# End of the up-projection: two chunks' biases and taps back to back, and the lows of down's second and third pair by subtraction instead of an accumulating transfer

## The chip, the cores and the metric

The kernel runs on one core of one Trainium2 chip. The metric is the device time of one execution in microseconds (us); for a comparison, the median of several runs. The engines are written as in the profile: PE is TensorE's matmul, PEld its weight load, DVE is VectorE, ACT is ScalarE, POOL is GpSimd, SP is SyncE, which here only issues DMAs.

## The reference

A decoder trunk of two layers over x of 512 tokens by 1024 features, in float32. Each layer is a mixer (dilated window attention in the first, forgetting attention in the second) and then a gated feed-forward block with a causal convolution. The change lies in that block, which runs once a layer:

```python
def conv_ffn(xn, w_up, cw, cb, w_down):       # w_up 1024 x 5632, w_down 2816 x 1024
    a = xn @ w_up
    T = a.shape[1]
    ap = jnp.pad(a, ((0, 0), (CONV_W - 1, 0), (0, 0)))           # CONV_W = 3
    a = sum(ap[:, j:j + T] * cw[j] for j in range(CONV_W)) + cb
    gate, val = jnp.split(a, 2, axis=-1)
    return (jax.nn.gelu(gate, approximate=True) * val) @ w_down
...
h = h + rms_norm(conv_ffn(rms_norm(h, g[2]), w_up[l], conv_w[l], conv_b[l], w_down[l]), g[3])
```

## The kernel before

**Products in two halves.** TensorE works on float32 numbers split in two: a *high* (the number rounded, made by a cast on ACT, `act.copy`) and a *low* (the number less its high). A product is three matmuls, high by high, high by low and low by high: lines 295, 296 and 297, in `mm3`. A low comes about in one of two ways. Either DVE subtracts the high from the raw tile (`pair_lows`, L836). Or ACT writes the negated rounded number (a scaled copy, L829) and POOL issues a DMA that adds the raw tile to it in place (L830).

**Up-projection.** The 5632 output features are 22 chunks of 128 gate features and 128 value features. Chunks 4 to 19 go in pairs by a scheme with seven products instead of eight; chunks 0 to 3, 20 and 21 go alone (`up`). A chunk's two results lie in two of the eight PSUM banks (`bank`, name "up"). Then, on the bank's results: ACT adds bias and the last tap (`biased` L657, or in `taps` L670), DVE adds the two other taps, two instructions for the gate and two for the value (`shifted`, L664), ACT takes the GELU of the gate (`glu`, L689), and POOL multiplies gate and value (`product`, L686) and stores the product in `hD` in DRAM. `product()` always works on the chunk whose GELU was issued last before it.

**Down-projection.** Its 22 chunks of input form 11 pairs, again in a scheme with seven products. For a pair j, `pair_load` fetches the stored products, `pair_sums` makes three sums of them on DVE (L817 to L819) and stores one, `pair_highs` makes three highs on ACT (L827; two tiles of weights "wraw" and one of activations "dact"), and `pair_lows` the three lows. `mul_one(j, bp)` is twelve matmuls into four banks (name "acc"). `down` runs pairs 0 and 1 for bp = 0, then for bp = 1, then pair 2, pair 3 and so on with both: 24 matmuls a pair. The first four "acc" banks are those of chunks 18 and 19, the next four those of chunks 20 and 21; a bank is free when DVE has made the last tap from it.

**What sets the order.** Each engine runs its own instructions in the order in which the code issues them, and waits for other engines by semaphores. The code of `ffn` is written in the order that is wanted. Pair 0 is prepared during the last chunks in pairs (`prepare_last`); pairs 1 and 2 between the products of the last two chunks, in the lines that the change touches; pair 3 and the later ones in `down`. In what follows "sums(2)" or "lows(1)" are the steps of `pair_sums(2)` and `pair_lows(1)`, and "taps 18" the four instructions of L664 for chunk 18.

Of the kernel before, what the change touches and what calls it, by code (L numbers as in the profile page):

```python
# [12 lines left out]
AF = mybir.ActivationFunctionType  # L13
ALU = mybir.AluOpType
# [7 lines left out]
NF = DFF // 128  # L22
# [93 lines left out]
def trunk_kernel(ctx, tc, x, norm_gains, w_qkv_a, w_o_a, w_q_b, w_o_b, kv_norm, w_kvf, b_f,  # L116
                 w_up, conv_w, conv_b, w_down, rope, out):
    nc = tc.nc
    act, dve, pool, pe, sp = nc.scalar, nc.vector, nc.gpsimd, nc.tensor, nc.sync
# [8 lines left out]
    def t8(shape, dt=F32, name="t8"):  # L128
        return p8.tile(shape, dt, tag="t8", name=name)

    def t4(shape, dt=F32, name="t4"):
        return p4.tile(shape, dt, tag="t4", name=name)

    def t2(shape, dt=F32, name="t2"):
        return p2.tile(shape, dt, tag="t2", name=name)

    def bank(shape, name="bank"):
        return psp.tile(shape, F32, tag="ps", name=name)
# [510 lines left out]
    def ffn(l, bd, cp, nxt, ahead):  # L649
# [4 lines left out]
        def biased(c, banks):  # L654
            bb = t4([128, 2, T], name="bb")
            for s, ch in ((0, c), (1, NF + c)):
                act.activation(bb[:, s, :], banks[s], AF.Identity, bias=cp[:, 3, ch:ch + 1],  # L657
                               scale=cp[:, 2, ch:ch + 1])
            return bb

        def shifted(c, banks, bb, s):
            ps, ch = banks[s], s * NF + c
            for n in (1, 2):
                dve.scalar_tensor_tensor(bb[:, s, n:], ps[:, :T - n], cp[:, 2 - n, ch:ch + 1], bb[:, s, n:],  # L664
                                         ALU.mult, ALU.add)

        def taps(c, banks, between=None):
            bb = t4([128, 2, T], name="bb")
            for s, ch in ((0, c), (1, NF + c)):
                act.activation(bb[:, s, :], banks[s], AF.Identity, bias=cp[:, 3, ch:ch + 1],  # L670
                               scale=cp[:, 2, ch:ch + 1])
                shifted(c, banks, bb, s)
                if s == 0 and between is not None:
                    between()
            return bb
# [3 lines left out]
        def product():  # L679

            if gated:
                c, bb = gated.pop()
                if c - 1 in hc:
                    pool.dma_start(hD[c - 1], hc.pop(c - 1))
                hc[c] = t2([128, T], name="hc")
                pool.tensor_tensor(hc[c], bb[:, 0, :], bb[:, 1, :], ALU.mult)  # L686

        def glu(c, bb):
            act.activation(bb[:, 0, :], bb[:, 0, :], AF.Gelu_apprx_tanh)  # L689
            gated.append((c, bb))  # L690

        def post(c, banks, between=None):
            product()
            glu(c, taps(c, banks, between))
# [90 lines left out]
        def prepare_last():  # L785

            for added in (False, True, False, False):
                W.high(added)
                (W.low_added if added else W.low)()
                yield  # L790
            pair_sums(0)
            yield
            pair_highs(0)
            pair_sums(1)
            yield
            pair_lows(0)
            yield
# [1 line left out]

        acts, one, two, raws, todo, later2 = {}, {}, {}, {}, {}, {}
        H = slice(0, 512), slice(512, 1024)
        a11, s1_, s3_, s2_ = (slice(i * 256, i * 256 + 256) for i in range(4))

        def pair_load(j):

            if j < ND:
                acts[j] = k = t8([128, 1024], name="dact")
                sp.dma_start(k[:, 0:512], hD[2 * j])  # L810
                sp.dma_start(k[:, s2_], hD[2 * j + 1, :, 256:512])

        def pair_sums(j):

            pair_load(j + 1)
            k = acts[j]
            dve.tensor_tensor(k[:, s3_], k[:, a11], k[:, s1_], ALU.subtract)  # L817
            dve.tensor_tensor(k[:, s1_], k[:, s1_], k[:, s2_], ALU.add)
            dve.tensor_tensor(k[:, s2_], k[:, s1_], k[:, a11], ALU.subtract)  # L819
            pool.dma_start(sD[j], k[:, s2_])  # L820

        def pair_highs(j, added=False):

            raws[j] = [*W.take(2), acts.pop(j)]
            one[j] = [t8([128, 2, 1024], F32R, name="w") for _ in range(3)]
            for w, r in zip(one[j], raws[j]):
                act.copy(w[:, 0], r)  # L827
                if added and r is not raws[j][2]:
                    act.activation(w[:, 1], r, AF.Copy, scale=-1.0)  # L829
                    pool.dma_start(w[:, 1], r, accum_op=ALU.add)  # L830
            todo[j] = slice(2 if added else 0, 3)

        def pair_lows(j):
            s = todo.pop(j)
            for w, r in zip(one[j][s], raws.pop(j)[s]):
                dve.tensor_tensor(w[:, 1], r, w[:, 0].bitcast(F32), ALU.subtract)  # L836

        def load_two(j):
# [68 lines left out]

        def down(nxt, ahead):
            pair_highs(3)
            for bp in range(2):  # L910
                for j in range(2):
                    mul_one(j, bp)
            for j in range(1, ND - 2):
                if j > 1:
                    mul_one(j, 0)
                    mul_one(j, 1)
                if j + 3 < ND:
                    pair_sums(j + 3)
                    pair_lows(j + 2)
                    pair_highs(j + 3)  # L920
                elif j + 3 == ND:
                    pair_lows(j + 2)
                    load_two(0)
# [58 lines left out]
        def up(w, o, kcs):  # L982
            wh, wl = (t.rearrange("p (k c) -> p k c", k=8) for t in w)
            for kc in kcs:
                bh, bl = xs(xT, kc, ALL)
                mm3(o, wh[:, kc, :], wl[:, kc, :], bh, bl, kc == 0, kc == KD - 1)
# [16 lines left out]
        before = None  # L1003
        for c in (2, 3):
            banks = [bank([128, T], name="up") for _ in range(2)]
            for s in range(2):
                up(W.get(), banks[s], range(KD))
                if s == 0 and before:
                    product()
                    bb = taps(*before)  # L1010
# [8 lines left out]
            before = c, banks  # L1019
# [10 lines left out]
        def begin(p):  # L1030

            banks = [[bank([128, T], name="up") for _ in range(2)] for _ in range(2)]
            times(p, "A11", [b[0][:, LO] for b in banks], True)
            return banks

        def keep_first(banks):
            s1 = t2([128, 2, 256], name="csum")
            for q, b in enumerate(banks):
                act.copy(s1[:, q], b[0][:, LO])
            return s1  # L1040
# [8 lines left out]
        pend = [(*before, 0, None, None)]  # L1049
        banks = begin(PAIRS[0])  # L1050
        s1 = keep_first(banks)
        for p in PAIRS:
# [16 lines left out]
            bbs = [biased(*pend[0][:2])]  # L1069
# [34 lines left out]
            pend = [(2 * p + q, banks[q], q, s1, s12) for q in range(2)]  # L1104
            if p + 1 in PAIRS:
                banks, s1 = later, keep_first(later)
# [3 lines left out]
        banks = [begun[1], bank([128, T], name="up")]  # L1110
# [1 line left out]
        begun = None  # L1112
        ends(pend)
        product()
        glu(pend[0][0], taps(*pend[0][:2]))
        pair_highs(1, True)
        up(W.get(), banks[1], range(KD))
        post(*pend[1][:2])
        pair_sums(2)
        before = NF - 2, banks  # L1120
        banks = [bank([128, T], name="up") for _ in range(2)]
        up(W.get(), banks[0], range(KD))
        product()
        glu(before[0], taps(*before, lambda: pair_lows(1)))
        up(W.get(), banks[1], range(KD))
        before = NF - 1, banks
        pair_highs(2, True)
        post(*before)
        pair_lows(2)
        pair_sums(3)  # L1130
        product()
# [443 lines left out]

    bd2 = SharedBoundary(load_gain(norm_gains[0, 3], "gain03"), gcol, "xk")
    ffn(0, bd, cp[0], bd2, 4)


# [69 lines left out]
    banks = {b: bank([128, 512], name="v_ps") for b in bd2.order}  # L1649
# [78 lines left out]
    banks = [bank([128, 512], name="v_ps") for _ in range(4)]  # L1728
# [131 lines left out]
    for n in range(N + 3):  # L1860
        live = n < N
        if live:
            j, i = units[n]
# [53 lines left out]


    ffn(1, bd, cp, Final(load_gain(norm_gains[1, 3], "gain13")), 0)


# [40 lines left out]
```

## Time and profile before

| what | value |
|---|---|
| median of 3 runs | 1095.73 us (1094.23 to 1095.74) |
| the profiled execution | 1095.56 us |
| its span, first to last instruction | 1093.8 us |
| mean granted TensorE clock over the span | 0.997 |
| busy: PE, PEld | 1082.7 us (99%), 958.0 us (88%) |
| busy: DVE, ACT, POOL | 888.1 us (81%), 703.5 us (64%), 320.7 us (29%) |
| end of the up-projection, first and second layer | about 386 to 402 us and 965 to 979 us from the span's start |

The page of the profile gives each engine's busy time as a share of the span. The other views used below are the list of waits (who waited for whom, how long in all, how often, the longest), the timeline of an engine (start, length, instruction, and in brackets the idle time before it with what ended it), and a table of busy times by stretches of time. Matmuls are pipelined, so their lengths overlap; the distance between two starts tells their pace. The TensorE clock is given as a share of the full one.

### The profile page before, as it was taken

The page shows a single profiled execution, that of the slowest core. Times are in us where ns is not written, and L with a number is a line of the kernel's source. Part 1 is how long each engine was busy: PE and PEld are TensorE (multiplying, and loading weights), DVE is VectorE, ACT ScalarE, POOL GpSimd, SP SyncE. Part 2 cuts the span into 40 slices and gives each one's busy share as a digit, 9 for nine tenths or more (in the row PEclk, how much of TensorE's full clock was granted, in tenths as well). Part 3 has the DMA queues.
Part 4 walks back from the last instruction along what each step waited for, and adds up shares of the span by engine and source line. Part 5 has one row for each costly group of instructions (what it writes and reads, how often), then busy time and mean ns, then how long its engine had stood idle before and what let it go on. Part 6 is the DMA issues. An engine that isn't in the chain of part 4 may idle for free.

```text
span 1093.8 us, 18994 instructions
## 1 busy us (share of the span) xinstructions
PE 1082.7 (99%) x6897; PEld 958.0 (88%) x6897; DVE 888.1 (81%) x1442; ACT 703.5 (64%) x1155; POOL 320.7 (29%) x338
## 2 busy tenths in 40 slices
PE   9999999999999999999999999999999999999997
PEld 7888889899999977888888888889899999987886
DVE  5898978679899879997686677858679999879995
ACT  6745666766776666576551677756766676757573
POOL 2643000364665542000001212100354565532000
PEclk9999999999999999999999999999999999999999
DMA  9899956898788989793447857775898788989862
GB/s 291 242 364 411 349 127 158 187 213 223 195 200 230 267 255 343 274 343 96 154 133 246 277 167 209 254 223 142 172 226 206 216 190 214 250 276 328 319 250 77
DMA packets 162677, 254.25 MB, mean 232 GB/s; under 512 B 13216, under 2 KB 106776, under 8 KB 162584
## 3 DMA queue, kind: packets, MB, share of 16 engines
q1 hardware_dynamic: 143784, 189.33, 52.1%
q0 software_dynamic: 18112, 63.71, 26.6%
q8 instruction: 54, 0.88, 0.3%
q14 instruction: 39, 0.32, 0.1%
q10 hardware_dynamic: 688, 0.01, 0.0%
HBM read 172.37 MB, written 39.73 MB: 194 GB/s over the span
## 4 chain that ended last, share of the span: by engine, by line
PE 90%; DMA 3%; issue 2%; ACT 2%; DVE 2%; POOL 1%; SPq 0%; DVEq 0%; ACTq 0%; POOLq 0%
PE up L295 11%; PE up L297 11%; PE up L296 11%; PE acc L295 8%; PE acc L297 8%; PE acc L296 8%; PE v_ps L295 2%; PE v_ps L296 2%; PE v_ps L297 2%; PE pT_ps L1803 2%; PE o_ps L1818 2%; PE s_ps L1769 2%; PE qk_ps L295 1%; PE first L295 1%; PE first L296 1%
## 5 line engine op out<-in xcount | busy, mean ns | idle before, releaser
L295 PE MATMUL up<-xsh,w 128*128 128x256 f32 x512 | 145.0, 283 | 0.0
L296 PE MATMUL up<-xsl,w 128*128 128x256 f32 x512 | 145.0, 283 | 0.0
L297 PE MATMUL up<-xsh,w 128*128 128x256 f32 x512 | 145.0, 283 | 0.0
L664 DVE SCALAR_TENSOR_TENSOR bb<-up,conv,bb 128x511 f32<-128x511 f32 (+1 forms) x160 | 118.6, 746 | 28.0 <-ACT bb L670 25.2
L736 ACT CAST w<-wraw 128x1024 fp32r<-128x1024 f32 x94 | 95.4, 1043 | 66.1 <-DVE wraw L764 44.8
L295 PE MATMUL acc<-w 128*128 128x512 f32 (+1 forms) x311 | 121.5, 391 | 3.1 <-DVE bb L664 3.1
L297 PE MATMUL acc<-w 128*128 128x512 f32 (+1 forms) x311 | 121.3, 390 | 0.3 <-DVE w L836 0.3
L296 PE MATMUL acc<-w 128*128 128x512 f32 (+1 forms) x267 | 104.1, 390 | 0.5 <-DMA w<-wraw 0.5
L686 POOL TENSOR_TENSOR hc<-bb 128x512 f32<-128x512 f32 x44 | 79.0, 1796 | 68.1 <-DVE bb L664 54.3
L297 PEld LDWEIGHTS up<-xsh,w 128*128 128x128 f32 x512 | 98.3, 192 | 0.0
L295 PEld LDWEIGHTS up<-xsh,w 128*128 128x128 f32 x512 | 98.3, 192 | 0.0
L296 PEld LDWEIGHTS up<-xsl,w 128*128 128x128 f32 x512 | 98.3, 192 | 0.0
L296 PE MATMUL up<-xbl,w 128*128 128x256 f32 (+1 forms) x256 | 79.3, 310 | 0.0
L295 PE MATMUL up<-xbh,w 128*128 128x256 f32 (+1 forms) x256 | 79.3, 310 | 0.0
L296 PE MATMUL up<-xcl,w 128*128 128x256 f32 (+1 forms) x256 | 79.3, 310 | 0.0
L295 PE MATMUL up<-xch,w 128*128 128x256 f32 (+1 forms) x256 | 79.3, 310 | 0.0
L297 PE MATMUL up<-xbh,w 128*128 128x256 f32 (+1 forms) x256 | 79.3, 310 | 0.0
L297 PE MATMUL up<-xch,w 128*128 128x256 f32 (+1 forms) x256 | 79.3, 310 | 0.0
L76 DVE TENSOR_TENSOR w<-wraw,w 128x1024 fp32r<-128x1024 f32 x50 | 60.1, 1221 | 17.6 <-ACT w L58 13.3
L58 ACT CAST w<-wraw 128x1024 fp32r<-128x1024 f32 x61 | 62.8, 1054 | 17.5 <-PE v_ps L296 6.9
L295 PEld LDWEIGHTS acc<-w 128*128 128x128 f32 x311 | 58.8, 189 | 16.4 <-issue 2.9
L297 PEld LDWEIGHTS acc<-w 128*128 128x128 f32 x311 | 58.8, 189 | 12.8 <-DVE w L836 0.7
(314 smaller groups left out, 3189.9 us busy)
## 6 DMA issues: line engine op xcount, KB each, us to landing
wraw<-in_w_up_dram SPq DMA_DIRECT2D x88, 512.0 KB
w<-wraw POOLq DMA_DIRECT2D x70, 512.0 KB, 5.2
dT<-dsums SPq DMA_DIRECT2D x28, 512.0 KB
dsums<-in_w_down_dram SPq DMA_DIRECT2D x22, 512.0 KB
dsums<-in_w_down_dram SPq DMA_DIRECT2D x44, 256.0 KB
hD<-hc POOLq DMA_DIRECT2D x44, 256.0 KB, 6.4
dact<-hD SPq DMA_DIRECT2D x44, 256.0 KB
wraw<-dT SPq DMA_DIRECT2D x22, 512.0 KB
```

The costliest lines, as they stand in the source:

```text
L58: (copy or self.nc.scalar.copy)(pair[:, 0], raw)
L76: self.nc.vector.tensor_tensor(pair[:, 1], raw, pair[:, 0].bitcast(F32), ALU.subtract)
L295: pe.matmul(o, ah, bh, start=first, stop=False, skip_group_check=shared)
L296: pe.matmul(o, ah, bl, start=False, stop=False, skip_group_check=shared)
L297: pe.matmul(o, al, bh, start=False, stop=last, skip_group_check=shared)
L664: dve.scalar_tensor_tensor(bb[:, s, n:], ps[:, :T - n], cp[:, 2 - n, ch:ch + 1], bb[:, s, n:], ALU.mult, ALU.add)
L686: pool.tensor_tensor(hc[c], bb[:, 0, :], bb[:, 1, :], ALU.mult)
L736: act.copy(w[a][:, 0], raw)
L1769: pe.matmul(sc[j, i][hh][:, :nn], qT[j][own, qp, i * 128:(i + 1) * 128], k[own, kp, :nn], start=qp + kp == 0, stop=qp == 1)
L1803: pe.transpose(o[:, k0 + k, :], p[:, hh, k * 128:(k + 1) * 128], ident)
L1818: pe.matmul(o[64 * hh:64 * hh + 64, i * 128:(i + 1) * 128], Vt[hd // 8][:, k, (hd % 8) * 64:(hd % 8) * 64 + 64], pT[j, i, hh][:, k, :], st ...
```

## The change

Three things are different, all in `ffn`, once for each layer.

The biases of chunks 18 and 19 (the last pair, in `pend`) are issued together, then the taps of 18, its GELU and its product, then those of 19; before, preparing pair 1 stood between the two chunks on ACT and POOL. Preparing pair 1 (`pair_highs(1)`) follows after both.

The lows of the weights of pairs 1 and 2 come from DVE's subtraction, as those of all other pairs do. Their scaled copies (four a layer on ACT) and accumulating DMAs (four a layer in POOL's queue) are gone, and DVE has four instructions of 128x1024 more. The option `added` and the list `todo` go with them.

All three lows of pair 1 stand on DVE after sums(2) and ahead of the taps of chunk 20; before, one low stood between that chunk's gate taps and value taps. Pair 2's highs are issued ahead of the last chunk's second product in the code; on ACT they stand between the GELU of chunk 20 and the biases of chunk 21, as before.

```diff
-        def pair_highs(j, added=False):
+        def pair_highs(j):
...
             for w, r in zip(one[j], raws[j]):
                 act.copy(w[:, 0], r)
-                if added and r is not raws[j][2]:
-                    act.activation(w[:, 1], r, AF.Copy, scale=-1.0)
-                    pool.dma_start(w[:, 1], r, accum_op=ALU.add)
-            todo[j] = slice(2 if added else 0, 3)
 
         def pair_lows(j):
-            s = todo.pop(j)
-            for w, r in zip(one[j][s], raws.pop(j)[s]):
+            for w, r in zip(one[j], raws.pop(j)):
                 dve.tensor_tensor(w[:, 1], r, w[:, 0].bitcast(F32), ALU.subtract)
...
         ends(pend)
         product()
-        glu(pend[0][0], taps(*pend[0][:2]))
-        pair_highs(1, True)
+        bbs = [biased(*e[:2]) for e in pend]
+        for e, bb in zip(pend, bbs):
+            for s in range(2):
+                shifted(*e[:2], bb, s)
+            glu(e[0], bb)
+            product()
+        pair_highs(1)
+        pair_sums(2)
         up(W.get(), banks[1], range(KD))
-        post(*pend[1][:2])
-        pair_sums(2)
+        pair_lows(1)
         before = NF - 2, banks
         banks = [bank([128, T], name="up") for _ in range(2)]
         up(W.get(), banks[0], range(KD))
-        product()
-        glu(before[0], taps(*before, lambda: pair_lows(1)))
+        post(*before)
+        pair_highs(2)
         up(W.get(), banks[1], range(KD))
-        before = NF - 1, banks
-        pair_highs(2, True)
-        post(*before)
+        post(NF - 1, banks)
         pair_lows(2)
         pair_sums(3)
         product()
```

In the built program of the first layer, ACT's instructions at this place stand as follows before the change. A bb tile is one chunk's biases and taps (4369 is chunk 18, 4419 chunk 19, 4463 chunk 20), and w_4382 to w_4384 are pair 1.

```order
L670 ACTIVATE bb_4369<-up_4040,conv_1644 128x512
L670 ACTIVATE bb_4369<-up_4041,conv_1644 128x512
L689 ACTIVATE bb_4369<-bb_4369 128x512
L827 CAST w_4382<-wraw_4304 128x1024
L829 ACTIVATE w_4382<-wraw_4304 128x1024
L827 CAST w_4383<-wraw_4307 128x1024
L829 ACTIVATE w_4383<-wraw_4307 128x1024
L827 CAST w_4384<-dact_4281 128x1024
L670 ACTIVATE bb_4419<-up_4042,conv_1644 128x512
L670 ACTIVATE bb_4419<-up_4043,conv_1644 128x512
L689 ACTIVATE bb_4419<-bb_4419 128x512
L670 ACTIVATE bb_4463<-up_4291,conv_1644 128x512
```

After it ACT has this at the same place, where chunk 19 is bb_4372, chunk 20 bb_4462, pair 1 is w_4396 to w_4398 and pair 2 begins with w_4475.

```order
L657 ACTIVATE bb_4369<-up_4040,conv_1644 128x512
L657 ACTIVATE bb_4369<-up_4041,conv_1644 128x512
L657 ACTIVATE bb_4372<-up_4042,conv_1644 128x512
L657 ACTIVATE bb_4372<-up_4043,conv_1644 128x512
L689 ACTIVATE bb_4369<-bb_4369 128x512
L689 ACTIVATE bb_4372<-bb_4372 128x512
L827 CAST w_4396<-wraw_4304 128x1024
L827 CAST w_4397<-wraw_4307 128x1024
L827 CAST w_4398<-dact_4281 128x1024
L670 ACTIVATE bb_4462<-up_4291,conv_1644 128x512
L670 ACTIVATE bb_4462<-up_4349,conv_1644 128x512
L689 ACTIVATE bb_4462<-bb_4462 128x512
```

The biases of chunk 19 moved up past five instructions of pair 1, of which two are gone, and pair 1's three casts moved behind the GELU of chunk 19.

DVE's instructions from the last one of sums(2) on stand as follows before the change; chunk 21 is bb_4514, and w_4384 and w_4503 are the activations of pairs 1 and 2.

```order
L819 TENSOR_TENSOR dact_4315<-dact_4315 128x256
L664 SCALAR_TENSOR_TENSOR bb_4463<-up_4291,conv_1644,bb_4463 128x511
L664 SCALAR_TENSOR_TENSOR bb_4463<-up_4291,conv_1644,bb_4463 128x510
L836 TENSOR_TENSOR w_4384<-dact_4281,w_4384 128x1024
L664 SCALAR_TENSOR_TENSOR bb_4463<-up_4349,conv_1644,bb_4463 128x511
L664 SCALAR_TENSOR_TENSOR bb_4463<-up_4349,conv_1644,bb_4463 128x510
L664 SCALAR_TENSOR_TENSOR bb_4514<-up_4434,conv_1644,bb_4514 128x511
L664 SCALAR_TENSOR_TENSOR bb_4514<-up_4434,conv_1644,bb_4514 128x510
L664 SCALAR_TENSOR_TENSOR bb_4514<-up_4435,conv_1644,bb_4514 128x511
L664 SCALAR_TENSOR_TENSOR bb_4514<-up_4435,conv_1644,bb_4514 128x510
L836 TENSOR_TENSOR w_4503<-dact_4315,w_4503 128x1024
L817 TENSOR_TENSOR dact_4427<-dact_4427 128x256
```

After it DVE has this behind the same instruction, with chunk 21 in bb_4508.

```order
L831 TENSOR_TENSOR w_4396<-wraw_4304,w_4396 128x1024
L831 TENSOR_TENSOR w_4397<-wraw_4307,w_4397 128x1024
L831 TENSOR_TENSOR w_4398<-dact_4281,w_4398 128x1024
L664 SCALAR_TENSOR_TENSOR bb_4462<-up_4291,conv_1644,bb_4462 128x511
L664 SCALAR_TENSOR_TENSOR bb_4462<-up_4291,conv_1644,bb_4462 128x510
L664 SCALAR_TENSOR_TENSOR bb_4462<-up_4349,conv_1644,bb_4462 128x511
L664 SCALAR_TENSOR_TENSOR bb_4462<-up_4349,conv_1644,bb_4462 128x510
L664 SCALAR_TENSOR_TENSOR bb_4508<-up_4436,conv_1644,bb_4508 128x511
L664 SCALAR_TENSOR_TENSOR bb_4508<-up_4436,conv_1644,bb_4508 128x510
L664 SCALAR_TENSOR_TENSOR bb_4508<-up_4437,conv_1644,bb_4508 128x511
L664 SCALAR_TENSOR_TENSOR bb_4508<-up_4437,conv_1644,bb_4508 128x510
L831 TENSOR_TENSOR w_4475<-wraw_4391,w_4475 128x1024
```

Two lows of pair 1 are new ahead of chunk 20's taps, the third moved up to them, and two lows of pair 2 (this one and the next) are new behind chunk 21's taps. PE has the same instructions in the same order.

More of the change, by code (lines that the diff above doesn't have):

```diff
@@ L797, in prepare_last @@
             yield
-        acts, one, two, raws, todo, later2 = {}, {}, {}, {}, {}, {}
+        acts, one, two, raws, later2 = {}, {}, {}, {}, {}
         H = slice(0, 512), slice(512, 1024)
```

## Prediction

> **What bounds the kernel now.** I read the engines' shares on the page first:
>
> ```profile
> PE 1082.7 (99%) x6897; PEld 958.0 (88%) x6897; DVE 888.1 (81%) x1442; ACT 703.5 (64%) x1155; POOL 320.7 (29%) x338
> ```
>
> TensorE (PE) runs all the time, so an edit that takes no matmul away can only win back what PE waits. The view of waits, for PE alone, shows where that is; the three rows below all lie at the end of the two up-projections, and "acc" is the first half of the down-projection:
>
> ```profile
> PE acc L295 <- DVE bb L664: 3.1, 4, 1.5
> PE acc L296 <- DMA w<-wraw: 0.5, 1, 0.5
> PE acc L297 <- DVE w L836: 0.3, 1, 0.3
> ```
>
> L664 is the taps: down's second set of banks is the memory of chunks 20 and 21, free once VectorE (DVE) has read them. L836 and the DMA make the lows of pairs 1 and 2. In PE's timeline (start, length, what; in brackets the idle time and what ended it) the first layer's rows are these, from the first matmul of down on:
>
> ```profile
> 401.56 0.39 PE L295 MATMUL acc<-w 128*128 128x512 f32 x1
> ...
> 408.14 0.39 PE L297 MATMUL acc<-w 128*128 128x512 f32 x1
> 409.17 0.47 PE L295 MATMUL acc<-w 128*128 128x512 f32 x1 [0.65 <-DVE bb L664]
> ...
> 410.61 0.47 PE L295 MATMUL acc<-w 128*128 128x512 f32 x1 [0.50 <-DVE bb L664]
> ...
> 415.72 0.50 PE L296 MATMUL acc<-w 128*128 128x512 f32 x1 [0.52 <-DMA w<-wraw]
> ```
>
> 401.56 to 408.14 is 29 steps, 0.227 us each, of matmuls that are 0.39 long: each starts 0.16 before the last one ends, so a stop loses its idle time and 0.16. The three lose 0.81, 0.66 and 0.68, and the longer matmul after each (0.47 to 0.50 for 0.39) holds its successor by another 0.08, 0.08 and 0.11: **2.43 us**. The second layer's rows:
>
> ```profile
> 978.43 0.39 PE L295 MATMUL acc<-w 128*128 128x512 f32 x1
> ...
> 982.02 0.50 PE L297 MATMUL acc<-w 128*128 128x512 f32 x1 [0.26 <-DVE w L836]
> ...
> 987.40 0.47 PE L295 MATMUL acc<-w 128*128 128x512 f32 x1 [1.46 <-DVE bb L664]
> ...
> 988.84 0.47 PE L295 MATMUL acc<-w 128*128 128x512 f32 x1 [0.51 <-DVE bb L664]
> ...
> 990.36 0.63 PE L296 MATMUL acc<-w 128*128 128x512 f32 x1
> 990.78 0.63 PE L297 MATMUL acc<-w 128*128 128x512 f32 x1
> ```
>
> The stops lose 0.42, 1.62 and 0.67, plus 0.27 for the restarts: 2.99. Then matmuls step by 0.42 instead of 0.23 (990.36 to 990.78). The table by stretches (length, then busy us of PE, PEld, DVE, ACT, POOL, and the granted clock) says why:
>
> ```profile
> 408.40:411.80 3.40, 2.25 (x9) 1.53 (x9) 3.37 (x5) 2.52 (x3) 0.49 (x1) 1.00 1.09 252
> 985.80:989.20 3.40, 1.44 (x6) 0.83 (x6) 3.33 (x5) 2.40 (x4) 1.32 (x2) 1.00 1.09 277
> 989.20:992.60 3.40, 3.40 (x10) 2.63 (x9) 3.26 (x8) 2.15 (x3) 0.35 (x1) 0.50 1.05 241
> ```
>
> After a stretch in which PE idled 1.96 of 3.4 us the clock was 0.50 for the next 3.4; after 1.15 idle (first layer) it stayed 1.00. At half the clock 3.4 us do the work of 1.7; less 0.1 at the edges I take 1.60, so the second layer loses **4.59 us**; both together 7.02, which is all that there is to win.
>
> **The change, part by part.** Per layer it takes four scaled copies off ScalarE (ACT) and four accumulating DMAs off POOL's queue, and gives DVE four lows more. Everything it moves lies on DVE and ACT ahead of down, so the question is when DVE delivers. DVE now:
>
> ```profile
> 387.95 2.97 DVE L664 SCALAR_TENSOR_TENSOR bb<-up,conv,bb 128x511 f32<-128x511 f32 x4 [0.24 <-ACT bb L670]
> 395.65 2.97 DVE L664 SCALAR_TENSOR_TENSOR bb<-up,conv,bb 128x511 f32<-128x511 f32 x4 [4.73 <-ACT bb L670]
> 398.54 0.42 DVE L817 TENSOR_TENSOR dact<-dact 128x256 f32<-128x256 f32 x1
> 399.80 1.53 DVE L664 SCALAR_TENSOR_TENSOR bb<-up,conv,bb 128x511 f32<-128x511 f32 x2
> 401.24 2.50 DVE L836 TENSOR_TENSOR w<-dact,w 128x1024 fp32r<-128x1024 f32 x1
> 407.49 2.98 DVE L664 SCALAR_TENSOR_TENSOR bb<-up,conv,bb 128x511 f32<-128x511 f32 x4 [2.31 <-ACT bb L670]
> 414.03 3.81 DVE L836 TENSOR_TENSOR w<-wraw,w 128x1024 fp32r<-128x1024 f32 x2
> 420.15 2.35 DVE L836 TENSOR_TENSOR w<-wraw,w 128x1024 fp32r<-128x1024 f32 x2
> 423.55 0.42 DVE L817 TENSOR_TENSOR dact<-dact 128x256 f32<-128x256 f32 x1
> ```
>
> Prices, from one start to the next: taps of a chunk 2.89 (395.65 to 398.54), the three sums 1.26 (398.54 to 399.80), three lows 3.40 (420.15 to 423.55). DVE idles 4.73 and 2.31 waiting for ACT, whose queue holds the pair's casts ahead of the biases. Two rows are longer than their kind, because of POOL's product of a chunk:
>
> ```profile
> 401.34 1.31 POOL L686 TENSOR_TENSOR hc<-bb 128x512 f32<-128x512 f32 x1
> ```
>
> It covers the low of 401.24, which takes 2.50 instead of some 1.2; so in 414.03, 3.81 instead of 2.35. A product that meets lows, or sums, which I take for the same kind, costs DVE 1.3 to 1.5; taps beside a product keep their 2.97 (395.65). ACT's prices:
>
> ```profile
> 387.14 1.45 ACT L670 ACTIVATE bb<-up,conv 128x512 f32<-128x512 f32 x2 [7.25 <-DVE up L1047]
> 389.58 0.63 ACT L689 ACTIVATE bb<-bb 128x512 f32<-128x512 f32 x1 [0.99 <-DVE bb L664]
> ...
> 409.66 1.99 ACT L827 CAST w<-wraw 128x1024 fp32r<-128x1024 f32 x2
> ```
>
> A GELU takes 0.6, a cast some 0.95 (two in 1.99), a bias some 0.7; taps start 0.81 after their first bias (387.14 to 387.95), the GELU 1.63 after the taps (to 389.58).
>
> The first layer, step by step in the new order:
> - Biases of 18 and 19 stand together from 387.14 to 389.8; taps 18 start at 387.95 as now, taps 19 follow at 390.85 with no wait, and end at 393.75. Second GELU 392.5, so pair 1's casts come at 393.1, to 395.9; now they stand behind the GELU of 389.58. That delay costs nothing: lows(1) start later.
> - sums(2) 1.26, lows(1) 3.40, and chunk 19's product, free at 393.9 and so beside them: 1.4. End 399.8. PE wants pair 1 from 401.56 + 13 × 0.227 = 404.5 on: the second layer's stop at 982.02 goes too.
> - Taps 20 399.8 to 402.7. Their GELU at 401.4, pair 2's casts 402.0 to 404.8, then the biases: taps 21 at 405.6 instead of 407.49, to 408.5. DVE idles 2.9 here, and chunk 20's product falls into that.
> - lows(2) to 411.9, sums(3) and sums(4) to 414.4, lows(3) 3.40 plus 1.46 for chunk 21's product as in the row of 414.03: last low 419.3.
>
> What PE wants, with no stop: chunk 21's gate bank for matmul 31 at 401.56 + 30 × 0.227 = 408.4, its value bank for matmul 34 at 409.05, pair 2's last low at 412.9, pair 3's at 401.56 + 74 × 0.227 = 418.3. It gets the banks 1.68 and 3.12 after taps 21 start (407.49 to 409.17 and to 410.61): 407.3 and 408.7, in time. Pair 2 is there 1.0 early. **Pair 3's last low is what is late next:** 419.4 for 418.34, a stop of 1.04 and 0.11 for the restart: 1.15 lost instead of 2.43. From pair 4 on DVE needs 1.26 + 3.40 a pair and PE 24 × 0.227 = 5.44, so it stays ahead.
>
> The second layer's DVE rows lie 578.22 later (its taps 18 below against 387.95), PE's only 576.87 (978.43 against 401.56): PE asks 1.35 earlier.
>
> ```profile
> 966.17 2.98 DVE L664 SCALAR_TENSOR_TENSOR bb<-up,conv,bb 128x511 f32<-128x511 f32 x4 [0.25 <-ACT bb L670]
> ```
>
> So in the first layer's time the gate bank is wanted at 407.0 (0.27 late, 0.35 with restart), the value bank at 408.0 (0.68, 0.76), pair 3's low at 418.1 (1.30, 1.41): 2.52 lost instead of 4.59, if the clock stays whole, since no stretch of 3.4 us holds two of the larger stops.
>
> Costed at nothing: the scaled copies and the DMAs that go (ACT is waited for only at taps 21, counted above; PE's one wait for the DMA is counted; the raw tiles that they read come free earlier, so SP's loads behind them move up, not down; POOL's products of 18 to 21 lose the four issues that stood ahead of them). A wait that is new in the order is that of pair 1's casts for the GELU of 19; behind it on ACT stand the biases of 20, at 395.9 instead of behind the taps of 19 now, and DVE asks for them at 399.8. Bounds of the unknown: the two holds by products cost 0 to 1.5 each; a clock halving 0 or 1.6 a layer.
>
> Sum: 2.43 − 1.15 + 4.59 − 2.52 = **3.35 us** off the profiled execution's span of 1093.8 and the 1.76 around it (1095.56), so 1092.2; the median of the runs is 0.17 above that execution: **1092.4 us**.
>
> By the Trainium skill ("TensorE: Matmul & The Clock Gate", "What's actually happening") the clock falls to half only after a whole idle window of some 3.4 us. This trace does not agree: PE was busy 1.44 us in the stretch ahead of the fall. By that rule the sum stays as it is and the first rival below has no chance.
>
> **Rivals.**
> - The clock halves again. It fell at 1.96 idle of 3.4 and held at 1.15; my stops are 1.15 (first layer), then 1.11 together and 1.41 (second). Any of these could lie past the point, or DVE be 0.5 later than worked out: 1.6 lost, 1094.0, which is within 0.2%. For it: 1.41 lies between the two. Against: it is nearer to 1.15. Chance 0.23.
> - No stop is left. If products held DVE for nothing, lows(3) would end 2.9 earlier, and 7.0 is won: 1088.7. For it: no row excludes that a product slips beside taps. Against: 401.24 and 414.03. Chance 0.10.
> - Slower: a third product, chunk 20's, falls not into DVE's idle 2.9 but on lows(2), and holds it 1.4. Then lows(3) end at 420.8, PE loses 2.55 and 3.9, each stop passes 1.96, and the clock halves in both layers: 2.55 + 1.6 + 3.9 + 1.6 = 9.65 against 7.02, so 1098.4. It decides from 1.2 us later than my 419.3. For it: every row of lows beside a product shows the hold. Against: the product could start at 402.9, and taps are not held. Chance 0.10.
>
> **How the numbers follow.** My forecast (1091 to 1093.5) has 0.57. A difference of 0.2%, 2.2 us, is about what a measurement of this kernel can tell from none. Faster: forecast and no stop, 0.67; same: 0.23; slower: 0.10. The range 1089.0 to 1095.0 leaves out half of the second rival and all of the third, 0.15.
>
> **What would show it.** Right: taps 18 and 19 without a gap on DVE; an idle of some 2.9 on DVE ahead of taps 21; PE's waits for L664 gone in the first layer and under 1 us in the second; a stop of 1 to 1.4 for pair 3's last low (L831 there, in the first matmuls after 417) in both; granted clock 1.00 throughout down. Wrong: a stop for pair 2's lows, a clock of 0.50 near 993, or casts that wait for raw tiles.

## Result and the profile after

The changed kernel took 1092.14 us, median of 8 runs (1090.90 to 1093.78). The kernel before, run beside it on the same chip, took 1094.64 us (8 runs, 1093.41 to 1096.89). The ratio is 0.9976, 95% interval 0.9965 to 0.9987: faster by some 2.5 us.

The profiled execution of the changed kernel is the slowest of its eight, 1093.78 us, with a span of 1092.0 us. The engines' shares and PE's list of waits, as shown of the kernel before:

```profile
PE 1080.9 (99%) x6897; PEld 956.8 (88%) x6897; DVE 890.7 (82%) x1450; ACT 694.5 (64%) x1147; POOL 312.0 (29%) x330
...
PE acc L297 <- DVE w L831: 1.6, 2, 1.1
PE pT_ps L1801 <- ACT prob L1779: 1.5, 1, 1.5
...
PE acc L295 <- DVE bb L664: 0.5, 1, 0.5
```

DVE has 8 instructions more (four lows a layer), ACT 8 fewer, POOL 8 fewer. Of the waits for taps (L664) one of four is left, the wait for the transfer is gone, and two waits for a low (L831) stand in their place. The second row is new, and lies neither in the up- nor in the down-projection: "pT_ps" are the transposes in the second layer's attention, some 177 us behind the end of the first layer's down (509.9 us).

DVE's timeline at the end of the first up-projection. This execution runs 0.99 us later at that point than the profile before (first matmul of down at 402.55 instead of 401.56):

```profile
389.04 5.86 DVE L664 SCALAR_TENSOR_TENSOR bb<-up,conv,bb 128x511 f32<-128x511 f32 x8 [0.24 <-ACT bb L657]
394.81 0.42 DVE L817 TENSOR_TENSOR dact<-dact 128x256 f32<-128x256 f32 x1
395.27 1.41 DVE L818 TENSOR_TENSOR dact<-dact 128x256 f32<-128x256 f32 x1
...
397.05 2.35 DVE L831 TENSOR_TENSOR w<-wraw,w 128x1024 fp32r<-128x1024 f32 x2
...
400.46 2.97 DVE L664 SCALAR_TENSOR_TENSOR bb<-up,conv,bb 128x511 f32<-128x511 f32 x4
406.26 2.98 DVE L664 SCALAR_TENSOR_TENSOR bb<-up,conv,bb 128x511 f32<-128x511 f32 x4 [2.83 <-ACT bb L670]
...
415.06 3.78 DVE L831 TENSOR_TENSOR w<-wraw,w 128x1024 fp32r<-128x1024 f32 x2
418.77 1.21 DVE L831 TENSOR_TENSOR w<-dact,w 128x1024 fp32r<-128x1024 f32 x1
```

Taps 18 and 19 are one row of eight without a gap; taps 21 wait 2.83 for their bias; the two lows of 415.06 take 3.78 where those of 397.05 take 2.35. PE's rows at the stops, first layer and then second:

```profile
402.55 0.39 PE L295 MATMUL acc<-w 128*128 128x512 f32 x1
...
420.03 0.50 PE L297 MATMUL acc<-w 128*128 128x512 f32 x1 [0.56 <-DVE w L831]
...
987.24 0.47 PE L295 MATMUL acc<-w 128*128 128x512 f32 x1 [0.52 <-DVE bb L664]
997.91 0.50 PE L297 MATMUL acc<-w 128*128 128x512 f32 x1 [1.09 <-DVE w L831]
```

And the stretch with the most idle time in down (length, then busy us of PE, PEld, DVE, ACT, POOL, granted clock, share of the DMAs, GB/s). PE idles 1.08 of 3.4 us and the clock stays whole:

```profile
994.50:997.90 3.40, 2.32 (x11) 1.58 (x9) 3.40 (x4) 3.08 (x4) 1.10 (x2) 1.00 0.59 223
```

In what follows "lost" is what the distances between the starts of the first 260 matmuls of a down exceed 0.227 us, summed. It is 7.02 before (2.43 in the first layer and 4.59 in the second) and 2.99 after (0.83 and 2.16).

### The profile page after: what moved, and what is told of

The parts are those of the page before. It is cut to its first block, busy times and chain, and to the rows that moved or that the text cites. A ratio compares the mean times of both kernels' runs of the same rounds, so it can differ in the third digit from the quotient of the medians.

```text
span 1092.0 us, 18966 instructions
## 1 busy us (share of the span) xinstructions
PE 1080.9 (99%) x6897; PEld 956.8 (88%) x6897; DVE 890.7 (82%) x1450; ACT 694.5 (64%) x1147; POOL 312.0 (29%) x330
## 4 chain that ended last, share of the span: by engine, by line
PE 88%; DMA 3%; DVE 3%; issue 2%; ACT 2%; SPq 1%; POOL 0%; DVEq 0%; ACTq 0%; POOLq 0%
PE up L297 12%; PE up L295 12%; PE up L296 12%; PE acc L297 8%; PE acc L295 8%; PE acc L296 8%; PE v_ps L295 2%; PE v_ps L296 2%; PE v_ps L297 2%; DVE w L831 2%; PE pT_ps L1801 1%; PE first L295 1%; PE qk_ps L295 1%; PE first L296 1%; PE first L297 1%
## 5 line engine op out<-in xcount | busy, mean ns | idle before, releaser
L664 DVE SCALAR_TENSOR_TENSOR bb<-up,conv,bb 128x511 f32<-128x511 f32 (+1 forms) x160 | 118.3, 746 | 19.6 <-ACT bb L670 16.2
```

## Experiments

All that follow were run beside the kernel before. "Attention" is the stop at the transposes in the second layer; "halved" is a granted clock of 0.50 within a down. These last three columns are those of the one profiled execution of each kernel.

| kernel | median us (runs) | ratio to before, interval | lost, layer 1 and 2 | attention | halved |
|---|---|---|---|---|---|
| changed kernel | 1092.14 (8) | 0.9976 [0.9965, 0.9987] | 0.83, 2.16 | 1.5 | no |
| e1_order_only | 1094.36 (11) | 0.9995 [0.9987, 1.0004] | 2.69, 3.32 | 0.3 | no |
| e2_lows_only | 1092.31 (10) | 0.9982 [0.9972, 0.9991] | 0.96, 1.69 | 1.7 | no |
| e3_biases_first | 1089.39 (5) | 0.9954 [0.9941, 0.9966] | 0, 0 | 1.7 | no |
| e4_two_products | 1093.72 (11) | 0.9991 [0.9982, 0.9999] | 1.78, 1.88 | 1.2 | no |
| e5_pool_11 | 1089.95 (5) | 0.9954 [0.9941, 0.9966] | 0, 0 | 1.3 | no |
| e6_pool_128 | 1089.90 (1) | | 0, 0 | 1.5 | no |
| e7_copies_out | 1088.49 (5) | 0.9940 [0.9928, 0.9952] | 0, 0 | 0 | no |
| e8_low_by_dve | 1088.09 (5) | 0.9938 [0.9924, 0.9951] | 0, 0 | 0 | no |
| e9_after_low | 1090.79 (5) | 0.9964 [0.9952, 0.9977] | 0.76, 1.47 | 0 | no |
| e10_before_low | 1093.71 (11) | 0.9992 [0.9984, 1.0001] | 2.46, 2.46 | 0 | no |
| e11_before_biases | 1104.31 (5) | 1.0089 [1.0076, 1.0103] | 7.76, 7.51 | 0 | both layers |
| b2_before_again | 1096.33 (1) | | 2.80, 4.45 | 0 | second |

**The two parts of the change apart.** e1_order_only has the new order, but the lows of the weights of pairs 1 and 2 are scaled copies with accumulating transfers as before:

```diff
-        pair_highs(1)
+        pair_highs(1, True)
...
-        pair_highs(2)
+        pair_highs(2, True)
```

> The new order of biases and taps alone; the lows of the weights of pairs 1 and 2 still come from scaled copies and accumulating transfers. Theory (what counts is when DVE delivers chunk 21's banks and the lows of pairs 1 to 3): ACT's four copies push the biases of chunk 21 back again, to about where they were in the kernel before, and pair 2's lows wait for a transfer again; lost at TensorE 1.7 to 2.7 us in the first layer and 3 to 4.5 in the second, against 0.83 and 2.16 in the changed kernel, so about 2.5 us slower than the changed kernel. Rival A (the back-to-back taps carry the gain): as fast as the changed kernel. Rival B (the transfers' absence carries it): as slow as the kernel before.

PE's waits in it:

```profile
PE acc L296 <- DMA w<-wraw: 3.9, 3, 1.6
PE acc L295 <- DVE bb L664: 0.8, 2, 0.5
```

The banks come earlier (0.8 instead of 3.1), and PE stands before the transfers instead (3.9 instead of 0.5). No gain can be measured. e2_lows_only is the reverse: the order of before, and DVE makes the lows.

```diff
-        pair_highs(1, True)
+        pair_highs(1)
...
-        pair_highs(2, True)
+        pair_highs(2)
```

> The subtraction for the lows of pairs 1 and 2 alone; biases and taps in the old order, pair 1's lows between the gate taps and the value taps of chunk 20. Theory: without the copies ACT reaches the biases of 19, 20 and 21 early enough, and pair 1's lows fall into the time in which DVE otherwise waits for chunk 21's biases; taps of 21 start as early as in the changed kernel, pair 1's lows come late by 0 to 0.5 us in the second layer; lost 0.8 and 2.2 us, total 3.0, so the changed kernel's time within 0.7 us. Rival A (the order carries the gain): as slow as the kernel before, 7.0 us lost. Rival B (the transfers' absence): the changed kernel's time.

It takes 1092.31: by itself it has the gain of the whole change, within the measurement. The order adds nothing that can be told apart on top of it.

**The stop that is left.** In the changed kernel chunk 21's product falls on the lows of pair 3. e3_biases_first lets ACT make chunk 21's biases ahead of pair 2's casts, so that its taps, GELU and product come earlier:

```diff
-        pair_highs(2)
         up(W.get(), banks[1], range(KD))
-        post(NF - 1, banks)
+        product()
+        bb = biased(NF - 1, banks)
+        pair_highs(2)
+        for s in range(2):
+            shifted(NF - 1, banks, bb, s)
+        glu(NF - 1, bb)
         pair_lows(2)
```

> The changed kernel with the two biases of chunk 21 ahead of pair 2's three casts on ACT. Theory: DVE's idle of 2.83 us ahead of the taps of 21 goes, everything behind it on DVE is 2.7 us earlier, pair 3's last low stands 2 us ahead of its matmul in the first layer and 0.7 in the second; lost 0 to 0.4 us in both together instead of 2.99, so about 2.8 us faster than the changed kernel. Rival (pair 3's lows hang on something else, its casts or its raw tiles): the stop at the 75th matmul stays, no gain over 0.8 us.

Nothing is lost in either down; DVE's idle time ahead of taps 21 is gone (taps 20 and 21 are one row), and pair 3's two lows are no longer held:

```profile
399.82 5.93 DVE L664 SCALAR_TENSOR_TENSOR bb<-up,conv,bb 128x511 f32<-128x511 f32 x8
...
413.37 2.35 DVE L831 TENSOR_TENSOR w<-wraw,w 128x1024 fp32r<-128x1024 f32 x2
```

It is 2.75 us below the changed kernel, for 2.99 lost there.

e4_two_products puts chunk 20's product also on the lows of pair 3, a lighter form of the third rival:

```diff
-        post(NF - 1, banks)
+        late = gated.pop()
+        glu(NF - 1, taps(NF - 1, banks))
         pair_lows(2)
         pair_sums(3)
+        gated.append(late)
+        last21 = gated.pop(0)
+        product()
+        gated.append(last21)
         product()
```

> The changed kernel with the product of chunk 20 behind sums(3), just ahead of that of 21, so that both fall on pair 3's lows: the slower rival of the prediction, made by hand. Theory: DVE is held 1.3 us more, the last low of pair 3 comes 1.3 us later, lost 2.1 us in the first layer and 3.5 in the second before any fall of the clock. If the clock falls at some 2 us idle of 3.4, as the trace before had it, each layer loses 1.6 more: 8.8 us in all, 5.8 us slower than the changed kernel. If it takes a whole idle window, 5.6 us in all, 2.6 slower. If products do not hold DVE: no change.

DVE's and POOL's rows:

```profile
414.45 4.86 DVE L831 TENSOR_TENSOR w<-wraw,w 128x1024 fp32r<-128x1024 f32 x2
...
414.67 1.31 POOL L686 TENSOR_TENSOR hc<-bb 128x512 f32<-128x512 f32 x1
416.88 1.35 POOL L686 TENSOR_TENSOR hc<-bb 128x512 f32<-128x512 f32 x1
```

Two products cost the two lows 2.51 (4.86 for 2.35), one costs 1.43 (3.78). In the first layer 0.95 more is lost than in the changed kernel, near what the second product adds (1.08). In all it is 3.66, not the 5.6 expected, and the time is 1.6 above the changed kernel's and not 2.6. In the second layer less is lost (1.88 for 2.16), which the hold doesn't explain. There DVE runs 0.10 us later against PE than in the first layer, in the changed kernel 1.36. That lag, which I had taken over from the kernel before as if it belonged to the layer, comes from this row of the changed kernel, a wait for a stored product that e4 hasn't got:

```profile
959.08 0.43 DVE L817 TENSOR_TENSOR dact<-dact 128x256 f32<-128x256 f32 x1 [1.39 <-DMA dact<-hD]
```

In the kernel before the lag has the same cause, two waits at these sums that the first layer hasn't got:

```profile
957.47 0.43 DVE L817 TENSOR_TENSOR dact<-dact 128x256 f32<-128x256 f32 x1 [0.40 <-DMA dact<-hD]
958.79 0.43 DVE L818 TENSOR_TENSOR dact<-dact 128x256 f32<-128x256 f32 x1 [0.90 <-DMA dact<-hD]
```

Why the transfer lands later in one kernel than in the other was not tried.

**What the landing cost, and what the traffic.** e11_before_biases is the kernel before with the edit of e3 alone, its transfers kept:

```diff
-        before = NF - 1, banks
-        pair_highs(2, True)
-        post(*before)
+        product()
+        bb = biased(NF - 1, banks)
+        pair_highs(2, True)
+        for q in range(2):
+            shifted(NF - 1, banks, bb, q)
+        glu(NF - 1, bb)
         pair_lows(2)
```

> The kernel before with chunk 21's two biases moved ahead of pair 2's casts and scaled copies on ACT, all else as it was (its lows of pairs 1 and 2 still come by transfers). Theory L (banks and landings were both late, and the one hides behind the other): the four stops for banks go, pair 2's transfers start 1.4 us later and TensorE comes 1.5 earlier, so it waits 2 to 3.5 us a layer for landings: 1094 to 1096, and a stretch of 3.4 us with over 1.96 idle may halve the clock (1.6 more). Rival (the biases queued behind casts were the whole cost): 3.8 less, some 1091.

```profile
PE acc L296 <- DMA w<-wraw: 9.0, 4, 3.0
...
418.57 0.79 PE L296 MATMUL acc<-w 128*128 128x512 f32 x1 [2.23 <-DMA w<-wraw]
```

The edit that wins 2.75 us without the transfers costs 9.8 with them (1104.31 for 1094.55). One part of this had been hidden: the list of waits of before puts the banks' stops at 3.1 against 0.5 for the transfer, but without a stop PE would want the second of pair 2's lows at 401.56 + 52 × 0.227 = 413.4 in the first layer, and the kernel before gets it at 415.72. That is 2.4 late, as much as the layer's three stops lose together (2.43), so better banks alone could have won nothing there. The other part is the edit's own: with the biases ahead of it ACT's scaled copy for this low starts 1.6 later (406.39 for 404.79), and the matmul stands until 418.57 where PE wants it at 413.6. Behind the stops (2.45 and 2.18 idle in the stretch ahead) the clock halved in both layers; 18 steps of 0.43 instead of 0.23 make 3.6 of the 15.3 us lost in the profile. Theory L named the wait, but not its size: it had 1094 to 1096, and 1.6 more for a fall of the clock. e7_copies_out is e3 with four transfers a layer of the same 512 KB put back, as copies to a scratch that nothing reads:

```diff
             for w, r in zip(one[j], raws[j]):
                 act.copy(w[:, 0], r)
+                if j in (1, 2) and r is not raws[j][2]:
+                    pool.dma_start(aside[2 * j - 2 + (r is raws[j][1])], r)
```

> e3_biases_first with four transfers of 512 KB a layer at the places where the kernel before issues its accumulating ones (pairs 1 and 2), here plain copies of the raw weights to a scratch in DRAM which nothing reads; no scaled copies on ACT. Theory L (the kernel before paid for landings that TensorE waited for, and for ACT's scaled copies, not for traffic): lost at TensorE in the two starts of down 0 to 0.5 us, time 1088.5 to 1089.6 (the transfer of e5 stands 415th in POOL's stream). Rival R (the traffic itself delays the loads of weights around it, or the raw tiles are held too long): 1.5 to 3 us lost in the two starts, time 1091 to 1092.5.

Nothing is lost in either down. So four more transfers of that size on POOL's queue cost nothing there; waiting for landings did, with the scaled copies that had to go ahead of them. Whether an accumulating transfer, which also reads its target, would be as free with nobody waiting was not tried. It is even 1.5 us faster than e5, which the next part explains.

**Where a part of the gain goes.** From the first matmul of the first down to that of the second the profiles show 576.87 us before and 576.50 after, though the first down alone lost 1.60 less. The stop at the transposes takes most of that back. In the rows of the changed kernel ACT's scaled copy of the last weights of the out-projection, POOL's transfer for it, DVE's next scores and PE:

```profile
677.23 1.09 ACT L69 ACTIVATE w<-wraw 128x1024 fp32r<-128x1024 f32 x1
679.53 0.90 POOL L96 DMA_DIRECT2D w<-wraw  x1 [10.81 <-ACT prob L1779]
685.94 0.29 DVE L1777 CUSTOM_DVE_ANT_0 prob<-s_ps,bias 128x128 f32<-128x128 f32 x1 [2.26 <-issue]
687.19 1.07 PE L1801 MATMUL pT_ps<-ident,prob 128*128 128x128 f32 x8 [1.45 <-ACT prob L1779]
```

The same in the kernel before, where PE doesn't wait:

```profile
677.94 1.09 ACT L69 ACTIVATE w<-wraw 128x1024 fp32r<-128x1024 f32 x1
679.33 0.86 POOL L96 DMA_DIRECT2D w<-wraw  x1 [9.89 <-ACT w L69]
684.96 0.29 DVE L1779 CUSTOM_DVE_ANT_0 prob<-s_ps,bias 128x128 f32<-128x128 f32 x1 [0.73 <-DMA w<-wraw]
```

DVE writes its scores into a buffer that held the raw weights, and so waits for the transfer that reads them. (The row of the changed kernel names no releaser, but the transfer issued at 679.53 takes 6.3 us to land, and DVE goes on 0.1 behind that; in the kernel before the row names it.) Before, that transfer is issued 0.30 us after the copy's end (679.03 to 679.33), after the change 1.21 (678.32 to 679.53). This 1.21 or 1.22 is in e2 to e6, in all of which the transfer is POOL's 82nd; in the kernel before and in e1 it is the 86th, and 0.30. The late issue is the larger part of the delay, not all: the transfer itself then took 6.3 from issue to landing, for 5.5 in the kernel before, and why is not shown.

e5_pool_11 and e6_pool_128 are e3 with 11 and 128 memsets of one element on POOL ahead of that attention, so that the transfer stands at another place among POOL's instructions:

```diff
     del wv
     next(down1)
+    spare = sml.tile([128, 1], F32, tag="spare", name="spare", bufs=1)
+    for _ in range(11):
+        pool.memset(spare, 0.0)
```

> e3_biases_first with 11 one-element memsets on POOL ahead of the second layer's attention; nothing reads them. They put the transfer of the out-projection's last low of weights back at the place in POOL's instruction stream that it has in the kernel before (416th instead of 405th). In e3 that transfer is issued 1.22 us after ACT's scaled copy, in the kernel before 0.30, and DVE, which needs the raw weights' buffer, and then TensorE (1.7) wait for its landing. Theory P (the late issue hangs on the place in POOL's stream): issued 0.30 after the copy, TensorE's stop 1.7 - 0.9 = 0.8 or less, time 1089.4 - 0.9 = 1088.5 (1087.6 to 1089.0). Rival T (it hangs on the times and transfers around it, which are as in e3): issued 1.2 after the copy, stop 1.7, time 1089.4.

> e3_biases_first with 128 of the same memsets: the transfer is 533rd in POOL's stream. Theory P, if what counts is the place within blocks of 128 instructions of 64 bytes (the 8192-byte packets of the instruction queue): issued 1.2 us after the copy again, stop 1.7, about 1089.4. Theory P with another length of block: 0.30 and about 1088.5. Rival T: 1.2, and then e5 shows 1.2 too.

Both show 1.22 and 1.21, and 1089.95 and 1089.90: the place among POOL's instructions isn't the cause, and theory P falls. The answer came from e7, which has four more transfers ahead but the same times:

```profile
650.86 1.09 ACT L69 ACTIVATE w<-wraw 128x1024 fp32r<-128x1024 f32 x1
653.20 0.91 POOL L96 DMA_DIRECT2D w<-wraw  x1 [10.81 <-ACT prob L1786]
...
675.67 1.09 ACT L69 ACTIVATE w<-wraw 128x1024 fp32r<-128x1024 f32 x1
677.06 0.89 POOL L96 DMA_DIRECT2D w<-wraw  x1 [9.84 <-ACT w L69]
```

Now the last transfer is on time (676.76 to 677.06), and the second of the four out-projection weights is late (651.95 to 653.20), where nobody waits for it. So the late issue goes with the transfers ahead on POOL's queue: it is the 82nd in e3, the 84th in e7. What DVE does meanwhile isn't the cause: from 0.5 us before the copy's end to 1.0 behind it, DVE starts the same instructions within 0.1 us in e7's last transfer, on time, and in e6's, late. If an accumulating transfer counts for two plain ones of its size, the count ahead is the same in both. By this count it should be the 81st in the kernel before, a store of "dsums", and that one does go 0.47 after its releaser (DVE ends at 609.57, issue at 610.04) where the 82nd goes after 0.30 (610.71, 611.01); the same holds in e1, e10, e11 and b2, with 0.46 or 0.47. This fits something in POOL's queue that turns over; what it is was not shown.

e8_low_by_dve takes the transfer away: DVE subtracts the last low.

```diff
-            W.minus()
-            W.low_added()
+            if j < 5:
+                W.minus()
+                W.low_added()
+            else:
+                W.low()
```

> e3_biases_first with the low of the out-projection's last weight in the second layer's attention subtracted by DVE (1.22 us) in place of ACT's scaled copy (1.09) and the accumulating transfer. In e3 DVE is idle 2.49 us there, until that transfer lands. Theory: TensorE's stop of 1.7 goes, DVE's 1.22 lies in its idle time, 1089.4 - 1.7 = 1087.7 (1087.2 to 1088.2). Rival: DVE comes late with the scores instead (1.22 against 0.81 idle ahead of them), TensorE stops 0.4 to 1.2 there: 1088.2 to 1089.

1088.09, 1.30 below e3. PE's only wait left is the first one of the program:

```profile
PE warm L249 <- DVE zero L244: 1.2, 1, 1.2
```

This version beats both kernels, the one before by 0.6% (ratio 0.9938, interval 0.9924 to 0.9951). e9_after_low and e10_before_low make the same edit in the changed kernel and in the one before.

> The changed kernel with e8's edit alone: the out-projection's last low in the second layer's attention by DVE instead of a scaled copy and a transfer. Theory G (the change's gain in the first layer is given back there, because with four transfers fewer ahead of it that transfer is issued 0.9 us late and TensorE stops 1.5): the stop goes, 1092.1 - 1.5 = 1090.6 (1090.0 to 1091.2), about 577.0 us less 2.0 between the first matmuls of the two downs, so near 575. Rival: the time between them is the same whatever the stop, another wait takes its place: 1091.8 to 1092.4.

> The kernel before with e8's edit alone. Theory G: that transfer is on time in the kernel before and TensorE doesn't wait there, so nothing is won: 1094.7 (1094.2 to 1095.2), within 0.05%. Rival (the transfer costs by itself, in both kernels): 1.0 to 1.7 less, 1093.0 to 1093.7. Its profile is a second look at before's second down: a clock of 0.50 after a stretch with 1.96 us idle of 3.4 there again if that much idle halves it every time, 1.00 if not.

In the changed kernel it wins 1.35, and the time between the two downs falls to 575.06: the stop was what gave the gain back. In the kernel before the ratio's interval holds 1, as theory G has it, but the median is 0.84 lower, below the range I gave and at the edge of the rival's (1093.0 to 1093.7). The kernel before has no stop in the attention to be won. The profile of e10 shows DVE in the second down without the lag (0.00 us against the first layer, 1.36 before; the waits of 957.47 and 958.79 are gone), with 2.46 lost for 4.59, and the clock whole. Whether the edit takes the lag away or the execution happened to have none is open.

**The clock.** b2_before_again is the kernel before, profiled once more.

> The kernel before, profiled once more. If 1.96 us idle in a stretch of 3.4 halves the clock each time: 0.50 in the second down again, 7.0 us lost in the two starts of down. If it was an event of that execution: 1.00 there, 5.4 lost. The attention of the second layer: no stop at the transposes, the out-projection's last transfer issued 0.30 after the scaled copy, both ways.

```profile
986.82:990.23 3.41, 1.53 (x6) 1.03 (x7) 3.34 (x5) 2.41 (x4) 1.09 (x1) 1.00 1.09 295
990.23:993.64 3.41, 3.41 (x10) 2.67 (x9) 3.27 (x8) 2.16 (x3) 0.60 (x2) 0.50 1.05 225
```

After 1.88 idle of 3.41 it halved again, so it was no event of one execution. Nor does every execution of the kernel before have it. 3.41 us at half the clock take 0.0016 off the mean granted clock of a run of 1094 us, and 23 of the 50 executions that ran beside the experiments have a mean of 0.999 or more, which leaves no room for such a stretch. Their median is 1094.2; that of the 12 with 0.997 is 1096.0.

## Why the prediction was right

The forecast was 1092.4 for the median, and 1092.1 came. That the two agree so closely is partly luck. I took 3.35 off a median of 1095.73, and the kernel before, run beside the changed one, had 1094.64; that base was 1.1 too high, and a stop that I had not seen, below, cost 1.2. On the profiled execution I was 1.6 too low (1092.2 for 1093.78). By its own steps:

- *Taps 18 and 19 without a gap, an idle of 2.9 ahead of taps 21, casts of pair 1 that cost nothing where they now stand:* as worked out (one row of 5.86; 2.83).
- *The hold by chunk 19's product, 1.4:* it fell on one of the sums, 1.41 for 0.43, so 1.0. The lows behind it take 2.35 and aren't held. This makes DVE 0.3 earlier than worked out.
- *Chunk 20's product in DVE's idle time:* there (POOL at 403.57, DVE idle until 406.26). With it the third rival falls.
- *Pair 3's last low is what is late next:* it is. The first layer loses 0.83 for 1.15, the 0.3 of the step above, and its stop is below the 1 to 1.4 that I had named as a sign. The second layer's terms were 0.35, 0.76 and 1.41 and measured 0.03, 0.76 and 1.37: 2.16 for 2.52.
- *The lag of the second layer, 1.35:* 1.36, and not because it belongs to the layer, as I had taken it: in both kernels DVE waits for the load of a stored product at the sums (959.08; 957.47 and 958.79 before). That the wait was there again is chance; in the other kernels the lag was −0.33 (e5) to 1.25 (b2).
- *The clock stays whole:* it did, with at most 1.09 idle of 3.41 in a down.
- *What stands elsewhere costs nothing:* here the working failed. I let the four transfers of a layer go at no cost but to free POOL and the raw tiles, and did not ask which later transfer on the same queue would now be late. The stop of 1.5 in the second attention was in no term and no rival. Net of 0.3 that the rows behind it win back it cost 1.2, and most of the first layer's gain (1.60) with it.

The sum of the profiled execution is then: 7.02 less 2.99 is 4.03 won, less 1.2 is 2.8, less the 1.0 by which this execution was already late ahead of the first down is 1.8, the difference of the spans (1093.8 to 1092.0). I had 3.35. The medians differ by 2.5, and that isn't explained term by term: the 1.0 at the start and the 1.60 for the clock in the kernel before are of single executions, and the clock's is missing in at least 23 of 50.

Of the rivals, "no stop is left" was not what this change gave, but e3 gives it, and 1089.4 there is 0.7 above the 1088.7 worked out for it, less than the stop of 1.7 in the attention that it keeps. The clock's rival is settled by a closer bound, below.

## What to carry to other kernels

A list of waits names what ended last, so a stop of 0.5 can stand for a transfer that is 2.4 late behind another wait; work out when the engine would have wanted it without the other stops before one pays for a new order. When a transfer is removed, follow its queue on to the next place where somebody waits for a landing or for a buffer that a transfer reads: here 1.2 us of the 1.6 won in the first layer were lost there. And ask of an engine's idle time what it could do instead of the late transfer: DVE, idle for 0.81, 1.27 and 2.49 us there in e3, did the low in 1.22.

## What the runs showed of the hardware that was not expected

- The granted clock. It halved after stretches of 3.41 us with 1.88 (b2), 1.96 (before), 2.18 and 2.45 us (e11) of PE idle. Ahead of the program's end it never did after 1.65 (e3, at the transposes) or less, in any of the profiles; at the end it held once more after 1.80 (e10) and fell after 1.93 (changed kernel, 1084.84 to 1088.25). The rows of e11, e3 and e10:

```profile
414.12:417.53 3.41, 0.97 (x3) 0.49 (x3) 3.38 (x5) 1.05 (x2) 0.93 (x2) 1.00 1.09 251
417.53:420.94 3.41, 2.37 (x6) 1.88 (x7) 3.38 (x5) 1.78 (x3) 0.54 (x1) 0.50 1.00 387
420.94:424.36 3.42, 3.42 (x10) 2.65 (x9) 3.35 (x6) 0.92 (x1) 0.54 (x1) 0.50 1.05 397
```

```profile
682.83:686.24 3.41, 1.76 (x11) 1.28 (x9) 1.18 (x7) 1.55 (x8) 0.00 (x0) 1.00 0.53 184
686.24:689.65 3.41, 3.37 (x36) 3.01 (x38) 3.34 (x15) 3.41 (x11) 0.77 (x2) 1.00 0.73 253
```

```profile
1083.98:1087.39 3.41, 1.61 (x12) 1.33 (x10) 2.96 (x8) 1.46 (x5) 0.00 (x0) 1.00 0.41 154
1087.39:1090.80 3.41, 0.00 (x0) 0.00 (x0) 0.86 (x2) 0.00 (x0) 0.00 (x0) 1.00 0.44 154
```

  In e11 it stayed halved for a second stretch after one with 1.04 idle, and came back after one that was busy throughout. The Trainium skill ("TensorE: Matmul & The Clock Gate", "What's actually happening") names an idle window of some 3.4 us for the fall; the length of the stretches agrees, 3.41, but a whole idle one was not needed in any of the four downs.
- One of the transfers that POOL issues for the out-projection's weights goes out 0.92 us later after its releaser than the other three (1.22 for 0.30). It is the same one in every kernel with the same transfers ahead of it; neither 11 nor 128 instructions more on POOL move it, and four transfers more do (e5, e6 and e7).
- A product of 128x512 on POOL holds an addition or subtraction of two SBUF operands on DVE by 1.0 to 1.5 us (1.41 for 0.43, 3.78 for 2.35), two products by 2.5 (4.86 for 2.35); taps, which read PSUM, keep their time beside it (2.97 in the kernel before at 395.65, with a product at 395.44).
